# Three raw weight buffers and eight 4 KB tiles, where there were two and ten, in a two-layer hybrid encoder trunk

## The chip, the cores and the metric

The kernel runs on one core of one Trainium2 chip. The metric is the time of one execution in microseconds as the device gives it; the median of three runs is quoted. Of one further execution there is a profile and a trace, and all rows below come from that one. TensorE (PE, with PEld for its weight loads), VectorE (DVE), ScalarE (ACT), GpSimd (POOL) and the DMA queues, nearly all of whose transfers are issued by SyncE (SP), work side by side, and wait for one another by semaphores.

## The reference

Two layers over 256 tokens of width 1024, in float32. Cut to what matters:

```python
def hybrid_layer(h, p_i, ...):
    u = rms_norm(h, g_mix_pre)
    (gq, gk, gv, gg, ra_f, ra_b, aq, ak, av, gate_a, gate_b) = split(u @ w_in)
    o_gla = rms_norm(gla(gq, gk, gv, decay(ra_f)) + gla_backward(gq, gk, gv, decay(ra_b)))
    branch_a = (o_gla * silu(gg)) @ w_o_gla                    # gated linear attention
    branch_b = attention(rope(rms_norm(aq)), rope(rms_norm(ak)), av) @ w_o_attn
    mixed = sigmoid(gate_a) * branch_a + sigmoid(gate_b) * branch_b
    h = h + rms_norm(mixed @ w_out, g_mix_post)
    gate, up = split(rms_norm(h, g_ffn_pre) @ w_ffn_in)        # hidden width 2816
    h = h + rms_norm((silu(gate) * up) @ w_ffn_out, g_ffn_post)
    e = p_i @ w_ple_proj
    return h + rms_norm(sigmoid(h @ w_ple_gate) * e, g_ple_post)
```

Nearly all of the work is in the products with weights, which are read once from memory and used for all 256 tokens.

## The kernel before

**Exactness by three passes.** Each float32 operand of a product is written as a sum of a high part (`wh` for a weight) in the matmul's own float32 format (`fp32r`) and a low part (`wl`), what the rounding left over. A product then is three matmuls: high by high, low by high, high by low (`passes`, line 123, and `mm`, line 107). To make the parts, `split` (line 135) issues two instructions: a copy with rounding on ScalarE (CAST) and a subtraction on VectorE. This holds for weights, and for activations when they have been turned so that the contracted dimension lies on the partitions (`transpose_in`, line 450, by TensorE, or `turn_out` and `take_in`, lines 461 to 474, by a DMA that transposes 16-bit halves, with a copy on ScalarE ahead of it and one behind).

**How weights are streamed.** A weight matrix is cut into units of 128 partitions by 2048 (or 2112) values, 1 MB each. The class `Stream` holds them in a fixed list in the order of use. `Load.start` takes a tile with tag `raw` from the pool `rawp` for a unit, and line 298 issues its DMA on the SP queue. When a unit comes up, `put` takes a `wh` and a `wl` tile from `wp` (four of each), and `fill` issues the casts and subtractions, in two halves of 128 x 1024; then `load` starts the next unit's DMA into a raw buffer. So a raw buffer is filled, cast and subtracted, and a new load into it waits for the subtraction that read it last. `take` gives the next ready pair to the matmuls; `done` gives its place back. At most four units are split and not used up.

Some blocks of weights (the second branch gate, and pairs of FFN blocks) are computed by a scheme of seven products for eight: sums of weight blocks are formed on VectorE (`step`). Their units lie in tiles of the pools `wp` (named `lent`) and `bigp`, not in `rawp`. The change leaves those pools alone.

**Pools.** On chip each partition has room for all pools together: `rawp` (8448 bytes a tile), `wp`, `bigp` (8 KB tiles, nine), `b4p` (4 KB tiles, ten, taken by `mid()`), `smp` (small tiles; four for each tag, where no number is given), and constants. In PSUM `accp` has eight tiles for sums. A tile of `mid()` serves for many things: the norms' scaled rows and squares, the gains that are loaded for them (line 373), the embedding's input `p` (line 1012), the rope table (lines 802 and 803, used by GpSimd in lines 807 to 812), decay weights (`up_weights`, line 828), operands of the linear and the softmax attention, the gated values, and the turned halves of the FFN's hidden activations.

**What sets the order.** The code is written stage by stage: start and rank projections (`0gla`, `0rq`), linear attention (`0gqk`, `0v`, `0gg`), gates and branch projections (`0gate`), merge and output projection (`0merge`, `0wout`), FFN (`0ffnin`, `0ffnout`), embedding (`0ple`), and the same for layer 1. The middle of a tile's name says in which stage it was made, and the first word which kind it is. A list scheduler puts the instructions of each engine and of the SP queue in order: by program order, by priorities (blocks under `high_priority`: the norms, the splits of activations), by its own estimates of when operands and buffers come free, and by explicit `issue_after`. The engines then take their list strictly in order. The number of buffers in a pool therefore changes not only who waits for whom, but also the lists.

**Norms.** `pre_norm` takes a norm ahead of a product: squares and sum (`row_rstd`), the factor 1/rms on GpSimd (lines 534 to 538), the product with the gain (line 542). `post_norm_add` is the norm behind a product: squares (line 522), factor, product with the gain (`vmul`, line 128), and the addition to `h` (line 609). `row_rstd` and `last_norm` each take a small tile `rstd`, of 4 bytes a partition. `outputs`, in the linear attention, takes a small tile `hss`, of 32 bytes. In the last part of an FFN the gated hidden values are made by `vmul` too, into tiles named `t_0ffnin` or `t_1ffnin`, and turned by TensorE or by the transposing DMA.

Of the kernel before, what the change touches and what calls it, by code (L numbers as in the profile page):

```python
# [61 lines left out]
def trunk_kernel(ctx: ExitStack, tc: tile.TileContext, a: dict, out: bass.AP):  # L62
# [8 lines left out]
    PSUM = bass.MemoryType.PSUM  # L71

    cp = ctx.enter_context(tc.tile_pool(name="cp", bufs=1))
    rawp = ctx.enter_context(tc.tile_pool(name="rawp", bufs=2))
    wp = ctx.enter_context(tc.tile_pool(name="wp", bufs=4))
    bigp = ctx.enter_context(tc.tile_pool(name="bigp", bufs=9))
    b4p = ctx.enter_context(tc.tile_pool(name="b4p", bufs=10))
    smp = ctx.enter_context(tc.tile_pool(name="smp", bufs=4))
    accp = ctx.enter_context(tc.tile_pool(name="accp", bufs=8, space=PSUM))

# [423 lines left out]
    def row_rstd(parts, behind=None):  # L504

        ss, r, junk = small(3, "ss"), small(1, "rstd"), mid() if parts[0].shape[-1] > 512 else t512()
        for j, src in enumerate(parts):  # L510
            n = src.shape[-1]
            if j == 2 and behind is not None:
                last_square[0] = nc.vector.scalar_tensor_tensor(
                    out=junk[:, :n], in0=src, scalar=1.0 / 1024.0, in1=src, op0=ALU.mult, op1=ALU.mult,
                    accum_out=ss[:, j : j + 1],
                )
                nc.vector.tensor_scalar(
                    out=r, in0=ss[:, 2:3], scalar1=ss[:, 0:1], scalar2=None, op0=ALU.add
                )
            else:  # L520
                with tc.issue_after(behind.ins) if j and behind is not None else nullcontext():
                    last_square[0] = nc.scalar.activation(
                        junk[:, :n], src, AF.Square, scale=1.0 / 32.0, accum_out=ss[:, j : j + 1]
                    )
            if len(parts) == 3 and j == 1:

                with in_turn():
                    last_pow[0] = nc.gpsimd.tensor_scalar(
                        out=ss[:, 0:1], in0=ss[:, 0:1], scalar1=ss[:, 1:2], scalar2=EPS if behind is not None else 0.0,
                        op0=ALU.add, op1=ALU.add,  # L530
                    )
        with in_turn():
            if behind is None or len(parts) == 2:
                nc.gpsimd.tensor_scalar(
                    out=r, in0=ss[:, 0:1], scalar1=ss[:, len(parts) - 1 : len(parts)], scalar2=EPS,
                    op0=ALU.add, op1=ALU.add,
                )
        last_pow[0] = nc.gpsimd.tensor_tensor(out=r, in0=r, in1=neghalf[:, 0:1], op=ALU.pow)
        return r
# [76 lines left out]
    def last_norm(parts, g, hf):  # L616

        with tc.high_priority(AHEAD):
            yt, junk, ss, r, c = mid(), mid(), small(3, "ss"), small(1, "rstd"), 0
            cuts = []  # L620
            for src in parts:
                cuts.append(slice(c, c + src.shape[-1]))
                c += src.shape[-1]
            nc.scalar.activation(junk[:, cuts[0]], parts[0], AF.Square, scale=1.0 / 32.0, accum_out=ss[:, 0:1])
            nc.vector.scalar_tensor_tensor(
                out=junk[:, cuts[1]], in0=parts[1], scalar=1.0 / 1024.0, in1=parts[1], op0=ALU.mult, op1=ALU.mult,
                accum_out=ss[:, 1:2],
            )
            with in_turn():
                nc.gpsimd.tensor_scalar(  # L630
                    out=ss[:, 2:3], in0=ss[:, 0:1], scalar1=ss[:, 1:2], scalar2=EPS, op0=ALU.add, op1=ALU.add
                )
            total = nc.vector.tensor_tensor_reduce(
                out=junk[:, cuts[2]], in0=parts[2], in1=parts[2], scale=1.0 / 1024.0, scalar=ss[:, 2:3],
                op0=ALU.mult, op1=ALU.add, accum_out=r,
            )
            nc.gpsimd.tensor_tensor(out=r, in0=r, in1=neghalf[:, 0:1], op=ALU.pow)
            yt = [acc(), yt[:, 0:256], acc()[:, 0:256]]
            for j, (src, c) in enumerate(zip(parts, cuts)):
                with tc.issue_after(total.ins) if j else nullcontext():  # L640
                    vmul(yt[j], src, g[:, c])
            for j, c in enumerate(cuts):
                x = h[:, hf, c]
                if j == 1:
                    nc.scalar.activation(yt[j], yt[j], AF.Copy, bias=0.0, scale=r)
                    nc.gpsimd.tensor_tensor(out=x, in0=yt[j], in1=x, op=ALU.add)
                else:
                    nc.vector.scalar_tensor_tensor(out=x, in0=yt[j], scalar=r, in1=x, op0=ALU.mult, op1=ALU.add)
                (nc.scalar if j == 1 else nc.sync).dma_start(out[0, hf * P : (hf + 1) * P, c], x)
# [397 lines left out]
    for l in range(DEPTH):  # L1047
# [332 lines left out]
        def outputs(hf, pr):  # L1380

            o = aux()
            ss = small(8, "hss")
            for i in range(2):
                hd = 2 * pr + i
                c = slice(hd * 256, (hd + 1) * 256)
# [402 lines left out]
```

## Time and profile before

| what | value |
|---|---|
| median of three runs (908.7, 910.29, 912.39) | 910.29 us |
| profiled execution: its time | 908.97 us |
| profiled execution: span, first to last instruction | 907.2 us |
| granted TensorE clock, mean | 0.997 |
| HBM read | 169.50 MB, 190 GB/s over the span |
| layers | layer 1's part is a repetition of layer 0's, less the start |

In the page of the profile a busy time is the time in which an engine worked on an instruction, and "idle before, releaser" tells how long the engine stood ahead of the instructions of a group, and what ended most of it. Rows that begin with two numbers come from a timeline: the first is the start in us from the beginning of the span, the second the time from there to the end of the last of so many instructions in a row (x4), and square brackets hold the wait ahead of them and what ended it. In rows of waits the three numbers are the total in us, the count and the longest. Rows of DMA groups end with the median time from issue to landing. Matmuls are pipelined, so that one can start before the one ahead of it has ended.

### The profile page before, as it was taken

How to read it: one execution, taken by the hardware profiler on the slowest of the kernel's cores; microseconds unless marked ns; L12 is line 12 of the kernel's file. 1: busy time of each engine (PE TensorE's matmuls, PEld its weight loads, DVE VectorE, ACT ScalarE, POOL GpSimd, SP SyncE). 2: the span in 40 equal slices, each digit the busy share in tenths (PEclk: the TensorE clock that was granted, in tenths of full speed). 3: DMA queues.
4: the chain of work that ended last, by engine and by line, in shares of the span. 5: the costliest groups of instructions: out<-in, count | busy, mean ns of one | idle time of the engine just before them, and what ended most of it. 6: DMA issues, size and time to landing. Idle time of an engine off the chain costs nothing.

```text
span 907.2 us, 12121 instructions
## 1 busy us (share of the span) xinstructions
PE 896.5 (99%) x4447; PEld 758.1 (84%) x4447; DVE 791.2 (87%) x1021; ACT 635.3 (70%) x1027; POOL 103.6 (11%) x157
## 2 busy tenths in 40 slices
PE   9999999999999999999999999999999999999997
PEld 8898888878888888877898888888888888888786
DVE  7999989987769989898779899799877799999984
ACT  6688679664569686666676687697645796958563
POOL 3700221300100000000244001110001000000001
PEclk9999999999999999999999999999999999999998
DMA  8654449657497685947575524475574966858461
GB/s 284 219 189 137 140 140 241 212 185 235 139 300 197 211 252 179 285 140 258 183 281 191 182 93 140 139 231 179 193 233 132 312 179 200 249 212 242 144 244 47
DMA packets 116967, 180.25 MB, mean 199 GB/s; under 512 B 30942, under 2 KB 55014, under 8 KB 116396
## 3 DMA queue, kind: packets, MB, share of 16 engines
q1 hardware_dynamic: 116748, 179.35, 61.4%
q8 instruction: 35, 0.57, 0.3%
q14 instruction: 24, 0.20, 0.1%
q10 hardware_dynamic: 160, 0.14, 0.0%
HBM read 169.50 MB, written 3.15 MB: 190 GB/s over the span
## 4 chain that ended last, share of the span: by engine, by line
PE 71%; DVE 14%; DMA 7%; issue 3%; ACT 3%; POOL 0%; POOLq 0%; SPq 0%; ACTq 0%; DVEq 0%
PE acc_1ffnin L123 10%; PE acc_1gate L123 7%; PE acc_0ffnin L123 5%; DVE wl_0ffnin L135 5%; PE acc_1ffnin L107 5%; DVE wl_0gate L135 3%; PE acc_1rq L123 3%; PE acc_0gqk L107 2%; PE acc_1gqk L107 2%; PE acc_1wout L123 2%; PE acc_0ple L123 2%; PE acc_1gg L123 2%; PE acc_1v L123 2%; PE acc_0v L123 2%; PE acc_1merge L123 2%
## 5 line engine op out<-in xcount | busy, mean ns | idle before, releaser
L135 ACT CAST wh_1ffnin<-raw_1ffnin 128x1024 fp32r<-128x1024 f32 x38 | 38.3, 1049 | 21.7 <-DMA raw_1ffnin<-in_w_ffn_out_dram 7.2
L135 DVE TENSOR_TENSOR wl_0ffnin<-raw_0ffnin,wh_0ffnin 128x1024 fp32r<-128x1024 f32 x38 | 44.7, 1221 | 8.5 <-ACT wh_0ffnin L135 8.4
L135 ACT CAST wh_0ffnin<-raw_0ffnin 128x1024 fp32r<-128x1024 f32 x38 | 38.0, 1047 | 19.6 <-DMA raw_0ffnin<-in_w_ffn_out_dram 11.1
L135 DVE TENSOR_TENSOR wl_1ffnin<-raw_1ffnin,wh_1ffnin 128x1024 fp32r<-128x1024 f32 x38 | 44.9, 1220 | 7.6 <-ACT wh_1ffnin L135 7.5
L107 PE MATMUL acc_0ffnin<-wh_0ffnin,big_0ffnin 128*128 128x512 f32 x176 | 45.4, 392 | 0.5 <-DVE big_0ffnin L135 0.5
L107 PE MATMUL acc_1ffnin<-wh_1ffnin,big_1ffnin 128*128 128x512 f32 x176 | 45.2, 390 | 0.0
L123 PE MATMUL acc_1ffnin<-wh_1ffnin,big_1wout 128*128 128x512 f32 x168 | 41.5, 389 | 0.0
L123 PE MATMUL acc_0ffnin<-wh_0ffnin,big_0wout 128*128 128x512 f32 x168 | 41.5, 389 | 0.0
L107 PEld LDWEIGHTS acc_0ffnin<-wh_0ffnin,big_0ffnin 128*128 128x128 f32 x176 | 32.7, 188 | 8.1 <-DVE big_0ffnin L135 0.9
L107 PEld LDWEIGHTS acc_1ffnin<-wh_1ffnin,big_1ffnin 128*128 128x128 f32 x176 | 33.0, 188 | 7.0
L123 PEld LDWEIGHTS acc_1ffnin<-wh_1ffnin,big_1wout 128*128 128x128 f32 x168 | 31.5, 188 | 6.6
L123 PEld LDWEIGHTS acc_0ffnin<-wh_0ffnin,big_0wout 128*128 128x128 f32 x168 | 31.5, 188 | 6.5
L135 DVE TENSOR_TENSOR wl_0ffnin<-lent_0ffnin,wh_0ffnin 128x1024 fp32r<-128x1024 f32 x30 | 35.7, 1220 | 0.6 <-ACT wh_0ffnin L135 0.6
L135 DVE TENSOR_TENSOR wl_1ffnin<-lent_1ffnin,wh_1ffnin 128x1024 fp32r<-128x1024 f32 x30 | 35.6, 1217 | 0.0
L135 ACT CAST wh_1ffnin<-lent_1ffnin 128x1024 fp32r<-128x1024 f32 x30 | 30.3, 1051 | 4.6 <-DVE lent_1ffnin L333 1.5
L135 ACT CAST wh_0ffnin<-lent_0ffnin 128x1024 fp32r<-128x1024 f32 x30 | 30.3, 1050 | 4.4 <-PE acc_0ffnin L123 1.6
L135 DVE TENSOR_TENSOR wl_0gate<-raw_0gate,wh_0gate 128x1024 fp32r<-128x1024 f32 x20 | 24.0, 1246 | 7.9 <-ACT wh_0gate L135 7.9
L135 DVE TENSOR_TENSOR wl_1gate<-raw_1gate,wh_1gate 128x1024 fp32r<-128x1024 f32 x20 | 23.6, 1220 | 7.3 <-ACT wh_1gate L135 7.3
L135 ACT CAST wh_0gate<-raw_0gate 128x1024 fp32r<-128x1024 f32 x20 | 19.8, 1046 | 12.8 <-DMA raw_0gate<-in_w_o_gla_dram 6.7
L135 ACT CAST wh_1gate<-raw_1gate 128x1024 fp32r<-128x1024 f32 x20 | 19.9, 1049 | 11.3 <-DMA raw_1gate<-in_w_o_gla_dram 4.7
L107 PE MATMUL acc_0ffnin<-wl_0ffnin,big_0ffnin 128*128 128x512 f32 x88 | 25.4, 399 | 1.4 <-DVE wl_0ffnin L135 1.4
L107 PE MATMUL acc_1ffnin<-wl_1ffnin,big_1ffnin 128*128 128x512 f32 x88 | 24.5, 395 | 0.6 <-DVE wl_1ffnin L135 0.6
(730 smaller groups left out, 2739.5 us busy)
## 6 DMA issues: line engine op xcount, KB each, us to landing
raw_0ffnin<-in_w_ffn_out_dram SPq DMA_DIRECT2D x11, 1024.0 KB, 6.4
raw_1ffnin<-in_w_ffn_out_dram SPq DMA_DIRECT2D x11, 1024.0 KB, 6.3
lent_0ffnin<-in_w_ffn_in_dram SPq DMA_DIRECT2D x6, 1024.0 KB
lent_1ffnin<-in_w_ffn_in_dram SPq DMA_DIRECT2D x6, 1024.0 KB, 9.0
raw_0v<-in_w_in_dram SPq DMA_DIRECT2D x4, 1024.0 KB, 5.1
raw_0gate<-in_w_o_gla_dram SPq DMA_DIRECT2D x4, 1024.0 KB, 5.9
raw_0gate<-in_w_o_attn_dram SPq DMA_DIRECT2D x4, 1024.0 KB, 5.0
raw_0wout<-in_w_ffn_in_dram SPq DMA_DIRECT2D x8, 512.0 KB, 6.3
```

Of the source, the lines that this page charges most:

```text
L107: return nc.tensor.matmul(o, lhsT, rhs, start=start, stop=stop)
L123: nc.tensor.matmul(o, x, y, start=start and n == 0, stop=stop and n == len(seq) - 1, **kw)
L135: return nc.scalar.copy(hi, src), nc.vector.tensor_tensor(out=lo, in0=src, in1=hi.bitcast(F32), op=ALU.subtract)
```

## The change

The pool of raw weight tiles has three buffers for two, 8448 bytes a partition more; the pool of 4 KB tiles has eight for ten, 8192 bytes less; the two small tags `rstd` and `hss` have two buffers for four. No instruction is added or taken out, and none has other operands than before, but for the buffers in which they lie.

```diff
-    rawp = ctx.enter_context(tc.tile_pool(name="rawp", bufs=2))
+    rawp = ctx.enter_context(tc.tile_pool(name="rawp", bufs=3))
...
-    b4p = ctx.enter_context(tc.tile_pool(name="b4p", bufs=10))
+    b4p = ctx.enter_context(tc.tile_pool(name="b4p", bufs=8))
...
# row_rstd
-        ss, r, junk = small(3, "ss"), small(1, "rstd"), mid() if parts[0].shape[-1] > 512 else t512()
+        ss, r, junk = small(3, "ss"), small(1, "rstd", 2), mid() if parts[0].shape[-1] > 512 else t512()
...
# last_norm
-            yt, junk, ss, r, c = mid(), mid(), small(3, "ss"), small(1, "rstd"), 0
+            yt, junk, ss, r, c = mid(), mid(), small(3, "ss"), small(1, "rstd", 2), 0
...
# outputs
-            ss = small(8, "hss")
+            ss = small(8, "hss", 2)
```

The order on the engines changes in many places. Three of them follow: rows with a minus stand there before, rows with a plus now, rows with neither in both.

The first is the SP queue in the gate stage of layer 0. `raw_0gate_...` are weight units (the number tells tiles apart), `mid_0gg_...` are transposed activations, `ggla` is a gain, and the rows L802 and L803 load the rope table; loads of gains and of `p` (L373, L1012) follow some rows further on, ahead of where raw_0gate_1890 stood.

```order
 L467 DMA_TRANSPOSE mid_0gg_1646<-big_0gg_1276 128x8x128 x2
-L298 DMA raw_0gate_1686<-in_w_o_gla_dram 128x4x512
+L298 DMA raw_0gate_1731<-in_w_o_gla_dram 128x4x512
 L373 DMA ggla_1gla_4912<-in_g_gla_out_dram 128x256
-L298 DMA raw_0gate_1731<-in_w_o_gla_dram 128x4x512
 L298 DMA raw_0gate_1803<-in_w_in_dram 128x4x512
+L298 DMA raw_0gate_1890<-in_w_o_gla_dram 128x4x512
 L802 DMA mid_0merge_2268<-in_rope_cos_dram 128x2x128
 L803 DMA mid_0merge_2268<-in_rope_sin_dram 128x2x128
```

Each weight unit stands one place earlier in the sequence of units: raw_0gate_1890 now comes before the rope table, where it came behind it and the loads that follow.

The second is the SP queue in the FFN of layer 0, at the last blocks of hidden values. `raw_` and `lent_` are weight units, and the transpositions turn the gated values for the output product.

```order
 L298 DMA raw_0ffnin_3376<-in_w_ffn_out_dram 128x2x1024
+L298 DMA raw_0ffnin_3396<-in_w_ffn_out_dram 128x2x1024
 L298 DMA lent_0ffnin_3390<-in_w_ffn_in_dram 128x4x512
 L298 DMA lent_0ffnin_3394<-in_w_ffn_in_dram 128x4x512
-L298 DMA raw_0ffnin_3396<-in_w_ffn_out_dram 128x2x1024
+L298 DMA raw_0ffnin_3445<-in_w_ffn_in_dram 128x4x512
 L467 DMA_TRANSPOSE t_0ffnin_3434<-mid_0ffnin_3155 128x8x128
-L298 DMA raw_0ffnin_3445<-in_w_ffn_in_dram 128x4x512
 L467 DMA_TRANSPOSE t_0ffnin_3460<-mid_0ffnin_3463 128x8x128
```

raw_0ffnin_3445 stood between the two transpositions and now stands ahead of both.

The third is VectorE at the end of the FFN of layer 1. `wl_` are subtractions for weight units, `t_1ffnin_...` are gated values that TensorE turns next, and `big_1ffnin_7700` are their low parts behind the turn.

```order
 L135 TENSOR_TENSOR wl_1ffnin_7601<-raw_1ffnin_7554,wh_1ffnin_7600 128x1024 x2
+L135 TENSOR_TENSOR wl_1ffnin_7633<-raw_1ffnin_7592,wh_1ffnin_7632 128x1024 x2
 L128 TENSOR_TENSOR t_1ffnin_7652<-mid_1ffnin_7458,t_1ffnin_7652 128x512
-L135 TENSOR_TENSOR wl_1ffnin_7633<-raw_1ffnin_7592,wh_1ffnin_7632 128x1024 x2
+L135 TENSOR_TENSOR wl_1ffnin_7656<-raw_1ffnin_7606,wh_1ffnin_7655 128x1024 x2
+L135 TENSOR_TENSOR big_1ffnin_7700<-aux_1ffnin_7695,big_1ffnin_7700 128x4x128
 L131 TENSOR_TENSOR mid_1ffnin_7457<-acc_1ffnin_7460,mid_1ffnin_7458 128x512
-L135 TENSOR_TENSOR big_1ffnin_7700<-aux_1ffnin_7695,big_1ffnin_7700 128x4x128
+L135 TENSOR_TENSOR wl_1ffnin_7680<-raw_1ffnin_7638,wh_1ffnin_7679 128x1024
 L128 TENSOR_TENSOR t_1ffnin_7676<-mid_1ffnin_7458,t_1ffnin_7676 128x512
-L135 TENSOR_TENSOR wl_1ffnin_7656<-raw_1ffnin_7606,wh_1ffnin_7655 128x1024 x2
```

The subtractions of one more weight unit now stand ahead of each of the two products t_1ffnin_7652 and t_1ffnin_7676.

## The prediction

> **What bounds the kernel now.** I read the page's busy line first, then the waits of TensorE, ScalarE and the SP queue, and last the timelines of the few places where TensorE really stands.
>
> ```profile
> PE 896.5 (99%) x4447; PEld 758.1 (84%) x4447; DVE 791.2 (87%) x1021; ACT 635.3 (70%) x1027; POOL 103.6 (11%) x157
> L107 PE MATMUL acc_0ffnin<-wl_0ffnin,big_0ffnin 128*128 128x512 f32 x88 | 25.4, 399 | 1.4 <-DVE wl_0ffnin L135 1.4
> PE acc_1ffnin L107 <- DVE wl_1ffnin L135: 0.6, 2, 0.4
> PE acc_0gate L123 <- ACT wh_0gate L135: 0.3, 1, 0.3
> ```
>
> TensorE is busy for 896.5 of the span's 907.2 us. No change to buffers takes a matmul out, so what can be won is only the time in which TensorE stands, and the rows show that to be small: 1.4 us of waits for `wl` in the FFN of layer 0, 0.6 us in layer 1, 0.3 us in the gate. But the end of a matmul is modelled here, with 0.399 us for one that can be followed much sooner, so idle time behind a matmul is understated. I count starts instead. Below, a block of five runs for 1.32 us; less the modelled 0.39 of the last, four steps of **0.23 us** are left, and what lies between two starts beyond 0.23 us per matmul is standing.
>
> ```profile
> SPq L298 <- DVE wl_0ffnin L135: 77.3, 19, 9.2
> ACT wh_0ffnin L135 <- DMA raw_0ffnin<-in_w_ffn_out_dram: 11.1, 3, 5.7
> ACT mid_0ffnin L474 <- DMA t_0ffnin<-mid_0ffnin: 6.2, 5, 2.7
> raw_0ffnin<-in_w_ffn_out_dram SPq DMA_DIRECT2D x11, 1024.0 KB, 6.4
> ```
>
> Two raw buffers do hold the loads back: in the FFN of layer 0 the SP queue waits 77.3 us, 19 times, for the subtraction that frees a buffer. Yet of that only 11.1 us reach ScalarE, as three waits for a landed unit, and 1.4 us reach TensorE. Cast and subtraction run ahead of the matmuls, and this lead swallows most late loads. So the question is local: where has the lead been used up?
>
> ```profile
> 182.75 0.61 PE L123 MATMUL acc_0gate<-wl_0gate,mid_0gate 128*128 128x512 f32 x2
> 183.62 1.68 PE L123 MATMUL acc_0gate<-wh_0gate,big_0gg 128*128 128x512 f32 x6 [0.25 <-ACT wh_0gate L135]
> ...
> 386.16 0.63 PE L107 MATMUL acc_0ffnin<-wl_0ffnin,big_0ffnin 128*128 128x512 f32 x2
> 387.04 0.74 PE L107 MATMUL acc_0ffnin<-wl_0ffnin,big_0ffnin 128*128 128x512 f32 x2 [0.25 <-DVE wl_0ffnin L135]
> 387.61 0.63 PE L107 MATMUL acc_0ffnin<-wh_0ffnin,big_0ffnin 128*128 128x512 f32 x2
> ...
> 399.64 0.84 PE L107 MATMUL acc_0ffnin<-wh_0ffnin,big_0ffnin 128*128 128x512 f32 x3
> 400.74 0.73 PE L107 MATMUL acc_0ffnin<-wl_0ffnin,big_0ffnin 128*128 128x512 f32 x2 [0.26 <-DVE wl_0ffnin L135]
> 401.87 0.73 PE L107 MATMUL acc_0ffnin<-wl_0ffnin,big_0ffnin 128*128 128x512 f32 x2 [0.40 <-DVE wl_0ffnin L135]
> 402.44 0.85 PE L107 MATMUL acc_0ffnin<-wh_0ffnin,big_0ffnin 128*128 128x512 f32 x3
> ...
> 415.64 1.16 PE L107 MATMUL acc_0ffnin<-wl_0ffnin,big_0ffnin 128*128 128x512 f32 x4
> 417.26 1.20 PE L107 MATMUL acc_0ffnin<-wh_0ffnin,big_0ffnin 128*128 128x512 f32 x4 [0.47 <-DVE big_0ffnin L135]
> ...
> 419.78 0.63 PE L107 MATMUL acc_0ffnin<-wl_0ffnin,big_0ffnin 128*128 128x512 f32 x2
> 420.67 0.73 PE L107 MATMUL acc_0ffnin<-wl_0ffnin,big_0ffnin 128*128 128x512 f32 x2 [0.26 <-DVE wl_0ffnin L135]
> ...
> 847.49 0.61 PE L107 MATMUL acc_1ffnin<-wh_1ffnin,big_1ffnin 128*128 128x512 f32 x2
> 848.26 0.73 PE L107 MATMUL acc_1ffnin<-wl_1ffnin,big_1ffnin 128*128 128x512 f32 x2 [0.16 <-DVE wl_1ffnin L135]
> 849.39 0.73 PE L107 MATMUL acc_1ffnin<-wl_1ffnin,big_1ffnin 128*128 128x512 f32 x2 [0.40 <-DVE wl_1ffnin L135]
> 849.96 1.32 PE L107 MATMUL acc_1ffnin<-wh_1ffnin,big_1ffnin 128*128 128x512 f32 x5
> ```
>
> Beyond 0.23 us a matmul, TensorE stands here for: gate 0.87 - 0.46 = 0.41; 386 to 387.6, four matmuls, 1.45 - 0.92 = 0.53; 399.6 to 402.4, seven, 2.80 - 1.61 = 1.19; 415.6, four, 1.62 - 0.92 = 0.70; 419.8, two, 0.89 - 0.46 = 0.43; layer 1, six, 2.47 - 1.38 = 1.09. Together **4.35 us**, 0.5% of the time: all that the larger waits on weights cost.
>
> The Trainium skill (Perfetto Trace Analysis, section Identifying Performance Opportunities) says that the same gap repeating on the engine that should be saturated can mean too little SBUF for the next tile. The trace agrees only for the SP queue, with its 19 waits; the gaps of TensorE do not repeat.
>
> **The change part by part.** *The third buffer* moves each load one unit earlier; the work is the same, and the gain is what the places above give up.
>
> ```profile
> 382.47 1.17 ACT L474 COPY mid_0ffnin<-t_0ffnin 128x1024 uint16<-128x1024 uint16 x1 [2.67 <-DMA t_0ffnin<-mid_0ffnin]
> ...
> 384.62 2.36 DVE L135 TENSOR_TENSOR wl_0ffnin<-raw_0ffnin,wh_0ffnin 128x1024 fp32r<-128x1024 f32 x2 [2.23 <-ACT wh_0ffnin L135]
> ```
>
> At 386 the root is not the weight unit itself. ScalarE waits 2.67 us for a turned tile whose transposition was issued behind a 1 MB load (raw_0ffnin_3445 between t_0ffnin_3434 and t_0ffnin_3460 in the order), VectorE therefore stands 2.23 us, and from there to 402 it has no time to catch up. In the changed order that load stands ahead of both transpositions and may start when the subtraction two units back is done, some 4 us sooner; the second transposition then no longer queues behind it. The casts and subtractions behind 382.47 come about 2 us sooner, more than the longest single hold-up of 0.6 us at 401.3, so 0.53 + 1.19 go. With the same lead the two units after 402 land before they are cast, and 0.70 + 0.43 go. In layer 1 the same pair of transpositions stands before 848: 1.09 goes. In the gate raw_0gate_1890 is issued at 176.0, after a run of small loads, and moves ahead of them: 0.41 goes. I take the whole **-4.35**.
>
> The Trainium skill (DMA: Bandwidth & Descriptors, section Queues, rings and completion order) says that each DMA engine takes the descriptors of a ring in order. By that rule the load now ahead of t_0ffnin_3434 could hold up that first transposition as it held up the second; the wait of 2.67 us agrees with the rule, and the second rival below is what it would give.
>
> *What is late next.* A cast and a subtraction that are ready sooner are also put ahead of other work.
>
> ```profile
> L135 ACT CAST wh_0ffnin<-raw_0ffnin 128x1024 fp32r<-128x1024 f32 x38 | 38.0, 1047 | 19.6 <-DMA raw_0ffnin<-in_w_ffn_out_dram 11.1
> L135 DVE TENSOR_TENSOR wl_0ffnin<-raw_0ffnin,wh_0ffnin 128x1024 fp32r<-128x1024 f32 x38 | 44.7, 1221 | 8.5 <-ACT wh_0ffnin L135 8.4
> ...
> 855.72 2.36 DVE L135 TENSOR_TENSOR wl_1ffnin<-raw_1ffnin,wh_1ffnin 128x1024 fp32r<-128x1024 f32 x2
> 858.00 0.68 DVE L128 TENSOR_TENSOR t_1ffnin<-mid_1ffnin,t_1ffnin 128x512 f32<-128x512 f32 x1
> ...
> 860.43 0.60 PE L450 MATMUL aux_1ffnin<-ident,t_1ffnin 128*128 128x128 f32 x4
> ```
>
> At the end of the FFN of layer 1 two more subtractions (wl_1ffnin_7633) now come before the product t_1ffnin_7652, which TensorE turns at 860.43. The subtraction row at 855.72 comes 0.9 us sooner with the rest, but the product then starts after 2 x 2.36 us of subtractions instead of one: 854.8 + 4.7 = 859.5, its end 860.2, against 860.43 - 1.09 = 859.3 at which TensorE now wants it: **+0.9**, and about +0.2 at the second turned half, which three more places of subtraction precede. In layer 0 the whole chain is 2.2 us sooner at this point, so the same two subtractions cost only about **+0.3**.
>
> *Eight 4 KB tiles for ten.* No row of before shows a wait for a 4 KB tile. In the changed program I find three new ones of any length.
>
> ```profile
> 147.48 1.89 DVE L135 TENSOR_TENSOR mid_0gate<-mid_0gate,mid_0gate 128x512 fp32r<-128x512 f32 x3
> ...
> 169.24 0.43 SPq L373 DMA_DIRECT2D mid_0wout<-in_g_ffn_pre_dram  x1
> 176.00 10.36 SPq L298 DMA_DIRECT2D raw_0gate<-in_w_o_gla_dram  x2
> 179.62 3.21 POOL L812 TENSOR_TENSOR rope_0merge<-mid_0merge 128x64 f32<-128x64 f32 x4
> ```
>
> The cast of mid_0gate_1701 must wait for the subtractions at 147.48 and is put six places later on ScalarE, into a stretch without idle time: 0.65 us of work there, of which I charge **+0.2** in each layer (nothing if the lead holds, 0.65 if none). The gain load mid_0wout_2287, at 169.24, must wait for GpSimd's last product, at 182.8, and stops the SP queue for 13.6 us. Behind it stand the load of `p` and the second raw_0gate, which before was issued at about 186 (176.00 + 10.36) anyway; raw_0gate_1890 stands ahead: 0. The zero fill for the next layer's decay weights comes 13.6 us later on GpSimd, and these are used more than 10 us after that: 0. Casts moved ahead of the attention's exponentials at 50 to 70 us find ScalarE idle, waiting for loads, but make two subtractions precede the scores' operands: I charge **+0.25** per layer (0 to 1.2, one subtraction).
>
> *The two-buffer small tiles* (`rstd`, `hss`) hold 4 bytes and 32 bytes a partition and are read within one norm; their previous user is over ten us back: 0, and one GpSimd instruction of some 0.6 us if not.
>
> **Sum:** -4.35 + 0.9 + 0.2 + 0.3 + 0.4 + 0.5 = **-2.05 us**, on the profiled execution 908.97 - 2.05 = 906.9 (span 907.2, with 1.8 us around it). The median of the runs, 910.29, lies 1.3 us above that execution and inside their spread of 908.7 to 912.39, so against the median I say **908.2**.
>
> **Rivals.** *The gain comes whole and more.* If the new costs vanish in other idle time, -4.35 is left, and with waits of the same kind under 0.2 us at other places (the 0.5 us for `big_0ffnin` is counted, the rest of the 907.2 - 896.5 is not) up to 6: about 905.2. For it: ScalarE stands 30% of the time. Against: VectorE, at 87%, is the one that releases TensorE in five of the six places. It is what the skill's rule on repeating gaps would give.
>
> *The wait only moves.* If the load that now leads holds up the first transposition as it did the second, the chain from 382 to 402, and its like in layer 1, start no sooner: 0.53, 1.19 and 1.09 stay, -1.54 + 2.3 = +0.8, 911.1. The same comes if the third buffer is filled no sooner because the SP queue itself is stopped. For it: the queue takes all in order, and a load takes 6.4 us to land. Against: the transposition is issued about 3 us after the load's new place.
>
> *Slower: weight work ahead of the norms.*
>
> ```profile
> 709.14 1.41 DVE L542 SCALAR_TENSOR_TENSOR mid_1wout<-h,rstd_1wout,mid_1wout 128x512 f32<-128x512 f32 x2 [0.85 <-POOL rstd_1wout L538]
> ...
> 709.94 0.66 PE L450 MATMUL aux_1wout<-ident,mid_1wout 128*128 128x128 f32 x4
> ```
>
> The first half of this norm ends at 709.14 + 0.75 and TensorE turns it at 709.94: nothing to spare. There are twelve such norms (after the output projection, the FFN and the embedding, two token halves, two layers). Each cast and subtraction that slips ahead of one costs 1.05 + 1.22 = 2.27 us less the chain's slack, and it decides from the point where that slack is under 2.27. With four norms hit it is +9.1 - 2.05, 917.3. Against: at 709 the casts that move ahead come out of ScalarE's way later (they ran before the squares already), so this one I find no later. For: the scheduler's order is set without these measured times.
>
> **How the numbers follow.** My forecast has a chance of 0.42, with a range of its own of 906 to 910.5; whole gain 0.18; moved wait 0.18; slower 0.22. A measurement of this kernel tells 0.5% from no change, 4.6 us here: faster is under 905.7, slower over 914.8. Most of the first rival and an edge of the forecast is faster: 0.19. Most of the slower rival is over 914.8: 0.2. The rest, 0.61, is within. The range of 8 in 10 must reach into both outer cases, and takes in the two bounds of the 0.65 and 1.2 us terms: 904.8 to 916.5.
>
> **What would show it.** Right: no idle time at 386 to 402 and 848, ScalarE's wait at L474 under 1 us, raw_0gate_1890 landed before 180; a new wait of TensorE for `t_1ffnin` at its turn near 860; the SP queue's waits for subtractions far under 77 us while TensorE's busy time stays. Wrong: TensorE waiting at L450 for a norm (slower), or ScalarE waiting at L474 for the first transposition (moved). The forecast fails if the chain of VectorE from 384 to 402 is as full as before and starts no sooner.

## The result, and the profile after

The changed kernel takes **906.3 us** (median of 13 runs, 904.55 to 907.59) against 910.29 us (median of 13 runs, 906.48 to 912.39): a ratio of 0.9965, with a 95% interval of 0.9951 to 0.9978 (the two medians alone give 0.9956, which lies inside it). That is 2 to 4.5 us less, a gain that is real and smaller than the 4.6 us that the prediction called its border. The forecast was 908.2: the direction and the range held, and the measured median lies 1.9 us under it.

The profiled execution took 906.67 us, its span is 904.9 us. The page and the groups by line answer the first rows that the prediction showed.

```profile
PE 895.2 (99%) x4447; PEld 760.0 (84%) x4447; DVE 789.9 (87%) x1021; ACT 634.9 (70%) x1027; POOL 105.0 (12%) x157
L107 PE MATMUL acc_0ffnin<-wl_0ffnin,big_0ffnin 128*128 128x512 f32 x88 | 24.1, 391 | 0.0
```

The same matmuls on `wl` that waited 1.4 us in all now wait for nothing. In the timeline of TensorE, the place from 399 to 402 runs without a break: the block of eight takes 1.98 us, and 1.98 less the last one's 0.39 is seven steps of 0.227.

```profile
400.68 1.07 PE L107 MATMUL acc_0ffnin<-wl_0ffnin,big_0ffnin 128*128 128x512 f32 x4
401.58 1.98 PE L107 MATMUL acc_0ffnin<-wh_0ffnin,big_0ffnin 128*128 128x512 f32 x8
```

What TensorE still waits for is in the table of its waits, and in this execution it is other things than weights. The second column is what it waited for, then the total in us, the count, the longest.

```profile
PE aux_1wout L450 <- DVE mid_1wout L542: 0.5, 1, 0.5
PE aux_1emb L1020 <- DMA mid_0ffnout<-in_p_dram: 0.4, 1, 0.4
PE acc_0rq L107 <- ACT wh_start L144: 0.4, 1, 0.4
PE acc_0gqk L107 <- DVE mid_0at L135: 0.2, 1, 0.2
```

The waits of the SP queue hold two surprises. Its waits for the subtractions of the FFNs are hardly shorter in layer 0 (77.3 us before) and longer in layer 1 (73.1 us before), and there is a new stop for GpSimd.

```profile
SPq L298 <- DVE wl_1ffnin L135: 83.0, 17, 14.5
SPq L298 <- DVE wl_0ffnin L135: 76.1, 20, 9.4
SPq L373 <- POOL rope_0merge L812: 11.5, 1, 11.5
```

To compare whole executions I take, for each of the 4447 matmuls and transpositions, the time from the start of the one ahead of it, and subtract the step that the same shape takes in a closed run (0.226 us for 512 columns, and in the same way for others). What is left, summed by stage, is the standing of TensorE. A step taken 0.001 us longer would make each total some 3.6 us smaller, so only the differences between columns count. Since one execution is little, each kernel has two: the runs `again` and `after_again` below are the same two kernels once more.

| standing, us | before | again | changed | after_again |
|---|---|---|---|---|
| start (0rq) | 0.93 | 1.62 | 2.00 | 1.57 |
| attention and decay operands, layer 0 (0gqk, 0at) | 0.57 | 0.57 | 1.51 | 1.53 |
| gates, layer 0 | 0.64 | 0.55 | 0.45 | 1.30 |
| merge, layer 0 | 0.59 | 0.76 | 0.23 | 0.18 |
| FFN, layer 0, and its end (0ffnin, 0ffnout) | 4.66 | 3.17 | 0.60 | 0.61 |
| embedding of layer 1 | 0.00 | 0.13 | 0.63 | 0.00 |
| output projection, layer 1 | 0.40 | 0.81 | 0.93 | 0.90 |
| FFN, layer 1 | 1.63 | 3.28 | 0.67 | 0.44 |
| all stages | 13.73 | 15.27 | 11.29 | 10.93 |

The two FFNs give 5.0 us (before against changed) and 5.4 us (again against after_again), all stages together 2.4 and 4.3 us. So 2.6 and 1.1 us are given back. The attention of layer 0 takes 0.95 us of that in both pairs. The rest lies in rows that differ by up to 0.85 us between two executions of the same kernel (the start, the gates, the embedding, the output projection), so two executions do not tell how much of it is the change's.

### The profile page after: what moved, and what is told of

Its sections match the earlier page's. It is cut to its first block, busy times and chain, and to the rows that moved or that the text cites. A ratio compares the mean times of both kernels' runs of the same rounds, so it can differ in the third digit from the quotient of the medians.

```text
span 904.9 us, 12163 instructions
## 1 busy us (share of the span) xinstructions
PE 895.2 (99%) x4447; PEld 760.0 (84%) x4447; DVE 789.9 (87%) x1021; ACT 634.9 (70%) x1027; POOL 105.0 (12%) x157
## 4 chain that ended last, share of the span: by engine, by line
PE 85%; DVE 6%; ACT 3%; DMA 3%; issue 2%; POOL 1%; SPq 0%; POOLq 0%; ACTq 0%; DVEq 0%
PE acc_0ffnin L123 12%; PE acc_1ffnin L123 11%; PE acc_1gate L123 7%; PE acc_1ffnin L107 7%; PE acc_0ffnin L107 6%; PE acc_1rq L123 3%; PE acc_1gqk L107 2%; PE acc_0wout L123 2%; PE acc_0v L123 2%; PE acc_1gg L123 2%; PE acc_1v L123 2%; PE acc_0merge L123 2%; PE acc_1merge L123 2%; PE acc_1ple L123 2%; PE acc_0gg L123 2%
## 5 line engine op out<-in xcount | busy, mean ns | idle before, releaser
L135 ACT CAST wh_1ffnin<-raw_1ffnin 128x1024 fp32r<-128x1024 f32 x38 | 38.6, 1049 | 17.4 <-PE acc_1ffnin L107 9.0
L135 ACT CAST wh_0ffnin<-raw_0ffnin 128x1024 fp32r<-128x1024 f32 x38 | 38.6, 1049 | 16.6 <-PE acc_0ffnin L107 7.6
L135 DVE TENSOR_TENSOR wl_0ffnin<-raw_0ffnin,wh_0ffnin 128x1024 fp32r<-128x1024 f32 x38 | 44.8, 1220 | 3.8 <-ACT wh_0ffnin L135 3.8
L135 DVE TENSOR_TENSOR wl_1ffnin<-raw_1ffnin,wh_1ffnin 128x1024 fp32r<-128x1024 f32 x38 | 44.8, 1220 | 2.4 <-ACT wh_1ffnin L135 2.4
L135 DVE TENSOR_TENSOR wl_1ffnin<-lent_1ffnin,wh_1ffnin 128x1024 fp32r<-128x1024 f32 x30 | 35.8, 1220 | 2.2 <-ACT wh_1ffnin L135 2.2
L135 DVE TENSOR_TENSOR wl_0ffnin<-lent_0ffnin,wh_0ffnin 128x1024 fp32r<-128x1024 f32 x30 | 35.7, 1219 | 1.6 <-ACT wh_0ffnin L135 1.6
L135 ACT CAST wh_1ffnin<-lent_1ffnin 128x1024 fp32r<-128x1024 f32 x30 | 30.6, 1049 | 8.5 <-PE acc_1ffnin L107 3.9
L135 ACT CAST wh_0ffnin<-lent_0ffnin 128x1024 fp32r<-128x1024 f32 x30 | 30.6, 1052 | 6.1 <-PE acc_0ffnin L107 3.9
L135 DVE TENSOR_TENSOR wl_0gate<-raw_0gate,wh_0gate 128x1024 fp32r<-128x1024 f32 x20 | 24.6, 1265 | 4.0 <-ACT wh_0gate L135 3.9
L135 ACT CAST wh_0gate<-raw_0gate 128x1024 fp32r<-128x1024 f32 x20 | 20.2, 1053 | 8.1 <-DMA raw_0gate<-in_w_o_attn_dram 3.5
L135 DVE TENSOR_TENSOR wl_1gate<-raw_1gate,wh_1gate 128x1024 fp32r<-128x1024 f32 x20 | 23.6, 1221 | 1.5 <-ACT wh_1gate L135 1.4
L135 ACT CAST wh_1gate<-raw_1gate 128x1024 fp32r<-128x1024 f32 x20 | 20.1, 1048 | 6.4 <-PE acc_1gate L123 3.5
```

The source lines that it names most:

```text
L135: return nc.scalar.copy(hi, src), nc.vector.tensor_tensor(out=lo, in0=src, in1=hi.bitcast(F32), op=ALU.subtract)
```

## The experiments

The theory was that in the FFNs a weight load stood between two transpositions in the SP queue and made the second late, and that the third buffer moves this load ahead. The rivals were: the third buffer's lead swallows late transpositions wherever the load stands; and the fewer 4 KB tiles do something of their own, for good or ill.

**again** is the kernel before, once more.

> The kernel before, unchanged, for a second profile of it: how far the places and lengths of TensorE's standing repeat from execution to execution. If the places are set by the order, the same six places show, each within 0.3 us of the first profile, and the span lies within 2 us of 907.2. If they come from the spread of the loads' landing times, other places show.

It took 910.58 us, span 908.5. The waits of TensorE on weights repeat in kind, not in place:

```profile
PE acc_1ffnin L107 <- DVE wl_1ffnin L135: 1.7, 3, 0.9
PE acc_0ffnin L107 <- DVE wl_0ffnin L135: 0.7, 2, 0.4
PE acc_0ffnin L107 <- DVE big_0ffnin L135: 0.5, 1, 0.5
```

The standing at 386 is not there, and there is one of 1.6 us at 789 in layer 1. Those at 184, 401, 416, 420 and 850 are. The norm at 709, which I had taken as free of waits, stands 0.5 us. The order of the instructions is the same in both, so it sets where TensorE can stand; where it does stand I put down to the spread of landing times (the load ahead of the second transposition landed at 381.43 in before and at 380.87 in again), which no run isolates. **after_again** says the same of the changed kernel:

> The changed kernel, unchanged, for a second profile. Standing that the change sets shows again at the same place: 56 (0.5 us), 196 (0.3 us), 438 (0.6 us), 863 (0.2 us), and none in the FFN from 386 to 421 and at 848. What the spread of landing times sets, at the start (5.5) and at the norm of layer 1 (708), may be longer or shorter by up to 1 us.

It took 906.23 us, span 904.5: 56 and 196 again, nothing in the FFN from 386 to 417 nor at 848, but not 438 nor 863, and 1.1 us at 197 where 0.3 had been.

**two_raw** takes the third buffer back and leaves the rest of the change:

```diff
-    rawp = ctx.enter_context(tc.tile_pool(name="rawp", bufs=3))
+    rawp = ctx.enter_context(tc.tile_pool(name="rawp", bufs=2))
```

> The changed kernel with two raw buffers in place of three, so that only the eight 4 KB tiles and the small tiles are left of the change. Theory A, the gain is the third buffer's alone and the fewer tiles cost next to nothing: within 0.6 us of before (ratio 0.9995 to 1.0007), TensorE stands at 386 to 402 and at 848 as before, and the SP queue's wait for the subtractions of layer 0's FFN stays near 77 us. Theory B, fewer 4 KB tiles bring part of the gain by another order: below before by 1 us or more (ratio under 0.999). Theory C, the eight tiles have a hidden cost that the third buffer covers: over before by 1 us or more.

It took **920.63 us**, ratio to before 1.0136 (1.0123 to 1.0149): theory C, by a size that I had not on my list. The loss is one place. In the FFNs nothing is gained: the SP queue waits 77.2 us for the subtractions of layer 0's, and TensorE waits 0.6 us for `wl` in layer 0 and 1.2 us in layer 1, so the fewer tiles alone do not remove those waits. The place is in the gate of layer 0. These are the SP queue, GpSimd, ScalarE and TensorE there, in the timeline of two_raw, and then three windows with the busy times of PE, PEld, DVE, ACT and POOL, the granted clock, and the share and GB/s of the DMA engines:

```profile
168.94 0.43 SPq L373 DMA_DIRECT2D mid_0wout<-in_g_mix_post_dram  x1
179.07 4.19 POOL L812 TENSOR_TENSOR rope_0merge<-mid_0merge 128x64 f32<-128x64 f32 x4
183.29 0.33 SPq L373 DMA_DIRECT2D mid_0wout<-in_g_ffn_pre_dram  x1
184.19 0.42 SPq L298 DMA_DIRECT2D raw_0gate<-in_w_o_gla_dram  x1
191.27 2.94 ACT L135 CAST wh_0gate<-raw_0gate 128x1024 fp32r<-128x1024 f32 x3 [15.39 <-DMA raw_0gate<-in_w_o_gla_dram]
192.36 2.08 PE L123 MATMUL acc_0gate<-wh_0gate,big_0gg 128*128 128x512 f32 x4 [8.96 <-ACT wh_0gate L135]
```

```profile
170.00:183.00 13.00, 13.00 (x59) 10.76 (x58) 12.97 (x10) 4.46 (x6) 9.67 (x10) 1.00 0.25 88
183.00:192.30 9.30, 0.41 (x2) 0.00 (x0) 0.12 (x1) 1.03 (x2) 0.26 (x1) 0.64 0.57 197
192.30:196.00 3.70, 3.64 (x9) 2.87 (x10) 3.66 (x4) 3.70 (x5) 0.00 (x0) 0.51 0.03 9
```

With eight tiles, the load of the FFN's pre-norm gain gets the tile of the rope table, and must wait until GpSimd has used it, at 183.3. The SP queue takes its list in order, so the weight load behind it, raw_0gate_1890, goes out at 184.19 and not at 176.00 as before; it lands at 191.2 (182.4 before), and TensorE stands 9 us. Behind that the clock is at 0.51 for 3.7 us, so that nearly half of it is lost as well, another 1.8 us (3.7 x 0.49). This is the stop that the prediction saw at 169.24 and priced at nothing, because raw_0gate_1890 stands ahead of it in the changed kernel.

**mid9** asks whether this needs any other order: it is the kernel before with nine tiles, and on every engine its list is that of before, row for row.

```diff
-    b4p = ctx.enter_context(tc.tile_pool(name="b4p", bufs=10))
+    b4p = ctx.enter_context(tc.tile_pool(name="b4p", bufs=9))
```

> The kernel before with nine 4 KB tiles in place of ten, nothing else; every engine has the same instructions in the same order as before, and the only difference is which earlier user a tile waits for. Theory A, one tile less is enough for the stop: the load of p (L1012) now waits for GpSimd's last rope product, and raw_0gate_1890 stands right behind it, so TensorE stands 8 to 10 us at about 192 and runs at half speed for 3 to 4 us behind it: 918 to 921, ratio 1.010 to 1.014. Theory B, the loss of two_raw came from its other order of casts and subtractions in the gate: no difference from before, ratio 0.999 to 1.001.

It took 917.99 us, ratio 1.0097 (1.0077 to 1.0117), just under the lower edge of what theory A had set, and far from theory B; TensorE stands 6.5 us where theory A had 8 to 10. Here it is the load of `p` that waits for GpSimd:

```profile
180.35 3.21 POOL L812 TENSOR_TENSOR rope_0merge<-mid_0merge 128x64 f32<-128x64 f32 x4
183.59 0.38 SPq L1012 DMA_DIRECT2D mid_0wout<-in_p_dram  x1
184.06 9.31 SPq L298 DMA_DIRECT2D raw_0gate<-in_w_o_gla_dram  x2
190.64 2.93 PE L123 MATMUL acc_0gate<-wh_0gate,big_0gg 128*128 128x512 f32 x6 [6.52 <-ACT wh_0gate L135]
```

One tile of 4 KB less, no instruction moved, 8.7 us lost. **unblock** then takes two_raw and puts only that gain load behind the weight load:

```diff
-        gpre = gain(a["g_ffn_pre"][l], mid(), D)
+        with tc.issue_after(sent[123].ins) if l == 0 else nullcontext(): gpre = gain(a["g_ffn_pre"][l], mid(), D)
```

(`sent[123]` is the DMA of raw_0gate_1890.)

> Two raw buffers, eight 4 KB tiles and the small tiles of the change, as in two_raw, but the load of the FFN's pre-norm gain of layer 0 is put behind the weight load raw_0gate_1890 in the SP queue, by an order constraint alone. Theory A, the loss of two_raw is one place: that gain load waits for GpSimd's rope products and stops the queue with the weight load behind it. Then the standing of 9.1 us at 192 in the gate goes, and with it the half-speed matmuls behind it (1.6 us): 920.6 - 10.7 = 909.9, ratio to before 0.9995 to 1.002. Theory B, eight tiles are short in many places: under half of the loss goes, the ratio stays over 1.006.

It took 910.91 us, ratio 1.0006 (0.999 to 1.0022): theory A, 1 us over what it had set. In this kernel's table TensorE's wait at the place is 0.7 us:

```profile
PE acc_0gate L123 <- ACT wh_0gate L135: 0.7, 1, 0.7
```

So the fewer tiles cost 10 to 12 us (by the medians and by the ratios) through one wait in one queue, and nothing that can be told elsewhere.

**between** keeps all of the change, but puts the one load of each FFN back between the two transpositions:

```diff
-                        nc.sync.dma_start(dst, src)
+                        with tc.issue_after(turns[-1].ins) if len(self.loads) in (84, 8) else nullcontext(): nc.sync.dma_start(dst, src)
```

(84 and 8 units are left when these two loads are issued; `turns[-1]` is the first transposition.)

> The changed kernel, three raw buffers, with one load a layer (raw_0ffnin_3445, raw_1ffnin_7360) put back between the two transpositions in the SP queue, by an order constraint alone. Theory A, the root in the FFN is a transposition that queues behind a 1 MB load: the second transposition lands 2 us or more later than in the changed kernel, ScalarE waits over 1.5 us for it at L474, and 1.5 to 2.8 us of the gain is lost (ratio to before 0.9985 to 0.9996). Theory B, the lead that the third buffer gives to all units swallows that wait: ScalarE waits at L474, but TensorE does not stand, and the time stays within 0.6 us of the changed kernel (ratio to before near 0.9965).

It took 906.33 us, ratio 0.9975 (0.996 to 0.9989): not to be told from the changed kernel, though the interval also reaches into theory A's range. The profile decides. The second transposition lands at 380.5 (378.3 in the changed kernel), and ScalarE waits 1.20 us for it at L474, less than the 1.5 us that theory A had set; the first row, 2.18 us, is a wait for the first transposition, whose copy now stands earlier in ScalarE's list. The timeline of between:

```profile
375.60 1.17 ACT L474 COPY mid_0ffnin<-t_0ffnin 128x1024 uint16<-128x1024 uint16 x1 [2.18 <-DMA t_0ffnin<-mid_0ffnin]
380.52 1.18 ACT L474 COPY mid_0ffnin<-t_0ffnin 128x1024 uint16<-128x1024 uint16 x1 [1.20 <-DMA t_0ffnin<-mid_0ffnin]
383.49 2.35 DVE L135 TENSOR_TENSOR wl_0ffnin<-raw_0ffnin,wh_0ffnin 128x1024 fp32r<-128x1024 f32 x2
```

In the changed kernel both copies run without a wait:

```profile
377.48 2.26 ACT L474 COPY mid_0ffnin<-t_0ffnin 128x1024 uint16<-128x1024 uint16 x2
```

But the subtraction behind them in between, at 383.49, has no wait ahead of it (2.23 us in the profile of before), and TensorE stands nowhere from 386 to 402. It does stand some 0.6 us more than in the changed kernel a little later, at 411.6 and 417.1, where it turns the gated values:

```profile
PE aux_0ffnin L450 <- DVE t_0ffnin L128: 0.3, 1, 0.3
```

My theory A falls here: of its 1.5 to 2.8 us at most 0.6 is there, so with three buffers the place of that load does not decide. Whether those 0.6 us come from the late transposition or from the spread is open.

**hold** is the other half: the kernel before, two buffers, ten tiles, and the load held back until the second transposition is issued.

```diff
-            while self.loads and (self.lend or
+            while self.loads and len(turns) >= held.get(len(self.loads), 0) and (self.lend or
...
-        nc.sync.dma_start_transpose(out=words.rearrange("p (x t) -> p x t", t=P), in_=planes)
+        turns.append(nc.sync.dma_start_transpose(out=words.rearrange("p (x t) -> p x t", t=P), in_=planes)); ws.start() if len(turns) in (13, 26) else None
```

(`held` is {85: 13, 9: 26}; the line with `issue_after` of between is in this kernel too.)

> The kernel before, two raw buffers and ten tiles, with the same one load a layer held back until the second transposition is issued. Theory A, the queue position of that load is the root: the wait of 2.67 us at L474 goes, the standing at 386 to 402 and at 848 goes with it (-1.7 and -1.1 us), 2 to 2.8 us under before (ratio 0.9969 to 0.998), with no third buffer. Theory B, the third buffer is needed because later loads are late too: the standing only moves to the next late unit (402 to 421 in layer 0), and under 1 us is won (ratio over 0.999).

It took 905.83 us, ratio 0.9975 (0.9961 to 0.9989): theory A. SP queue, ScalarE and the load, in the timeline of hold; the second transposition lands at 377.7 where it had been 382.4:

```profile
371.15 4.69 SPq L467 DMA_TRANSPOSE t_0ffnin<-mid_0ffnin  x2
375.88 0.58 SPq L298 DMA_DIRECT2D raw_0ffnin<-in_w_ffn_in_dram  x1
376.57 2.38 ACT L474 COPY mid_0ffnin<-t_0ffnin 128x1024 uint16<-128x1024 uint16 x2
```

By the rows of the table, the standing of the two FFNs falls to 0.66 and 0.58 us, with two buffers. The edit reaches beyond the SP queue: the scheduler also put the second copy (L474) right behind the first on ScalarE, with the split behind it, and moved a low part on VectorE. What hold shows is the new place together with this, not the place alone. One new wait takes 1.7 us of the gain in the profiled execution:

```profile
PE aux_1emb L1020 <- DMA mid_0ffnout<-in_p_dram: 1.7, 1, 1.7
```

**hold_late** turns `p` two ticks later for that (`embed(l + 1, 5)` for `embed(l + 1, 3)`).

> The kernel hold, two raw buffers and ten tiles with one load a layer behind the second transposition, and the turn of p for layer 1's embedding two ticks later. Theory A, the 1.8 us at 438 in hold are a wait for the load of p alone, and go: 1 to 1.8 us under hold, ratio to before 0.9955 to 0.9975. Theory B, the wait moves to the next turn: no difference from hold.

It took 906.55 us, ratio 0.9979 (0.9963 to 0.9994). The wait is gone from the profile, but the time is not to be told from hold's; in its profiled execution the start alone stands 1.2 us more than in hold's (2.80 and 1.64 us). The price of that wait stays open.

**big8** has the third buffer with all ten 4 KB tiles, and pays with one of the 8 KB tiles:

```diff
-    bigp = ctx.enter_context(tc.tile_pool(name="bigp", bufs=9))
-    b4p = ctx.enter_context(tc.tile_pool(name="b4p", bufs=8))
+    bigp = ctx.enter_context(tc.tile_pool(name="bigp", bufs=8))
+    b4p = ctx.enter_context(tc.tile_pool(name="b4p", bufs=10))
```

> Three raw buffers with all ten 4 KB tiles; the space comes from the pool of 8 KB tiles, which has eight in place of nine. Theory A, the third buffer makes the whole gain and the fewer 4 KB tiles only cost: no stop of the SP queue for GpSimd in the gate of layer 0, TensorE stands at none of the FFN places, time 905 to 906.5 (ratio to before 0.9945 to 0.9975). Theory B, a pool of 8 KB tiles that is one short costs in its place: new waits for big tiles, ratio over 0.999.

It took 905.79 us, ratio 0.9965 (0.9951 to 0.9978): theory A. The queue has no stop for GpSimd, the standing of the gate is 0.00 and that of the FFNs 0.58 and 0.66 us. The attention of layer 0 still stands 1.33 us, and in two_raw, with eight tiles and two buffers, it stands no longer than in before, so that price comes with the third buffer and not with the fewer 4 KB tiles.

**combined** and **keys_first** try to better the changed kernel by order alone: combined puts the gain load of the FFN's norm behind two weight loads and the turn of `p` three ticks later, keys_first also gives the splits of queries and keys a priority.

```diff
-        gpre = gain(a["g_ffn_pre"][l], mid(), D)
+        with tc.issue_after(sent[121].ins) if l == 0 else nullcontext(): gpre = gain(a["g_ffn_pre"][l], mid(), D)
...
-            embedding = embed(l + 1, 3)
+            embedding = embed(l + 1, 6)
```

The second part is in keys_first alone, and stands there for the keys in the same way:

```diff
-                split(qh, ql, ps)
+                with tc.high_priority(100): split(qh, ql, ps)
```

> The changed kernel with two of its new waits taken out by order alone: the load of the FFN's pre-norm gain of layer 0 goes behind two weight loads, so that its wait for GpSimd stops no weights, and the turn of p for layer 1's embedding is put three ticks later. Theory A, these waits are on TensorE's path: the standing at 196 (0.4 us) and at 438 (0.2 to 0.6 us) goes, 0.6 to 1.0 us under the changed kernel, ratio to before 0.9945 to 0.997. Theory B, they are covered elsewhere or come back at the next place: no difference from the changed kernel that can be told.

> The kernel combined, and the splits of the attention's queries and keys under a priority, so that their low parts come ahead of weight subtractions on VectorE. Theory A, the standing of 0.5 to 0.8 us at 55 to 60 is the price of weight subtractions put ahead of the scores' operands, and goes: 0.6 us under combined, ratio to before 0.994 to 0.9965. Theory B, the subtractions that are put back are late in their turn, and TensorE waits for wl in the projections at 50 to 70: no gain or a loss.

combined took 904.87 us, ratio 0.9957 (0.9943 to 0.9972), the lowest median of all. Its profile has neither wait (standing 0.00 in the gate and at the embedding, 9.32 in all), but its interval overlaps that of the changed kernel, so the gain is seen in the profile and not in the times. keys_first took 905.01 us, ratio 0.9954 (0.9939 to 0.9969): no gain over combined. The wait at 56 is gone, and this is what came for it:

```profile
PE acc_0v L123 <- DVE mid_0at L135: 1.2, 1, 1.2
```

It is again a low part of the attention, one stage on (theory B had expected a weight's).

## Why the prediction was right, and where it was not

**The bound** was right: no matmul went, and all that moved is the standing of TensorE.

**The -4.35 for the third buffer.** In the FFNs I had 2.85 us in layer 0 and 1.09 in layer 1, from the larger waits of one execution. By the sums of the table the two executions of before stand 4.66 and 3.17 us there in layer 0, and 1.63 and 3.28 in layer 1; after the change 0.6 and 0.4 to 0.7 are left. So the term of the FFNs is -5.0 to -5.4, not -3.94: I had counted one execution, and only its larger breaks. The 0.41 of the gate did not go. raw_0gate_1890 landed at 173.4 (I had said before 180), but the next unit, the second raw_0gate of the prediction's row at 176.00, then stands behind the stop for GpSimd and lands at 195.2, and TensorE stands 0.3 us at 196 for it, and 1.1 us in after_again.

**Its mechanism in the FFN** was half right. The load now stands ahead of both transpositions, the second lands at 378.3 and not at 382.4, and ScalarE's wait of 2.67 us is gone. By the Trainium skill (DMA: Bandwidth & Descriptors, section Queues, rings and completion order) that load could have held up the first transposition. The trace agrees that it lands behind the load, at 377.4 after 376.6; but in the kernel before it had a load ahead of it as well and landed at 377.9, so nobody waited longer, and this rival did not come here. A long wait for a transposition is there at the first one of each FFN, where it costs nothing. ScalarE's waits in the changed kernel:

```profile
ACT mid_0ffnin L474 <- DMA t_0ffnin<-mid_0ffnin: 4.6, 3, 3.7
ACT mid_1ffnin L474 <- DMA t_1ffnin<-mid_1ffnin: 3.5, 3, 2.8
```

The longest of layer 0 ends at 318.70 (the same copy waited 0.37 us before), that of layer 1 at 763.48. TensorE stands for neither: a wait longer than the 2.67 us of 382 has no price there. But `between` shows that three buffers don't need the new place, and `hold` that the new place, with the order that the scheduler made for it, doesn't need three buffers. Either of the two frees VectorE's chain at 384.

**The +0.9, +0.2 and +0.3 at the ends of the FFNs** were too much: 0 at the first turn of layer 1, at most 0.2 at the second, and none at the first turn of layer 0. The step that failed is "the subtraction row at 855.72 comes 0.9 us sooner with the rest". VectorE and TensorE in the changed kernel:

```profile
852.27 4.63 DVE L135 TENSOR_TENSOR wl_1ffnin<-raw_1ffnin,wh_1ffnin 128x1024 fp32r<-128x1024 f32 x4
856.82 0.69 DVE L128 TENSOR_TENSOR t_1ffnin<-mid_1ffnin,t_1ffnin 128x512 f32<-128x512 f32 x1
857.66 0.60 PE L450 MATMUL aux_1ffnin<-ident,t_1ffnin 128*128 128x128 f32 x4
```

The four subtractions do stand ahead of the product, but they begin 3.45 us sooner, and the product ends at 857.5, just in time. I had let VectorE gain only as much as TensorE, though its own wait for the late cast (1.17 us at 832.14 before) was gone as well.

**The +0.4 for casts in the gates** was 0: the gate of layer 1 stands 0.00 us.

**The +0.5 for the attention** had the right mechanism and the wrong shape: 0.95 us more in layer 0, nothing in layer 1. VectorE has four subtractions in a row there, and the low parts of the queries come behind them. The first two rows are from before, where one subtraction precedes the first low part, the other three from the changed kernel:

```profile
48.74 1.22 DVE L135 TENSOR_TENSOR wl_0kv<-raw_0rq,wh_0kv 128x1024 fp32r<-128x1024 f32 x1
49.88 0.68 DVE L135 TENSOR_TENSOR mid_0at<-aux_0at,mid_0at 128x512 fp32r<-128x512 f32 x1
49.80 4.62 DVE L135 TENSOR_TENSOR wl_0kv<-raw_0rq,wh_0kv 128x1024 fp32r<-128x1024 f32 x4
54.34 0.69 DVE L135 TENSOR_TENSOR mid_0at<-aux_0at,mid_0at 128x512 fp32r<-128x512 f32 x1
56.00 0.73 PE L107 MATMUL acc_0gqk<-big_start,wh_0kv 128*128 128x512 f32 x2 [0.21 <-DVE mid_0at L135]
```

**The sum.** By the means of the table the change is worth -3.4 us: -5.2 in the FFNs, +0.95 in the attention, and some +0.9 in rows that vary from execution to execution, such as the embedding (0.63 us in one execution, 0.00 in the other), for which the prediction had no term. Its gain of 4.35 was too small. Its costs of 2.3 are near the 1.8 or so that came back, but half of that came at places that it had not named, and the ends of the FFNs, with 1.4 of the 2.3, cost next to nothing; that the costs agree in total is luck.

**The stop of the SP queue, priced at 0,** was nearly right for the changed kernel, where it costs the 0.3 to 1.1 us at 196, and hid its largest number. Without the third buffer it costs 10 to 12 us; the third buffer pays for it by having one more unit on its way. By the ratios (1.0136 and 0.9965) the change is a loss of 12 us and a gain of 15 to 16, most of which meet in one place, and "0" was the difference of the two. The prediction named the wait, what was queued behind it, and why it did not count, and should have priced it with that cover gone.

**The rivals.** The whole gain and more, 4.35 to 6 us, had the size of what the FFNs give (5.0 to 5.4), but the costs did not vanish. Weight work ahead of the norms (slower) was not to be excluded by my argument: at 708 TensorE stands 0.6 us in both executions of the changed kernel. In before it is 0 in the first execution and 0.5 us in the second, so at most a part of it is the change's.

**What would show it.** The sign that failed is "the SP queue's waits for subtractions far under 77 us". They are 76.1, and in layer 1 they grew from 73.1 to 83.0. My reading, which no run isolates, is that a queue that loads ahead as far as buffers allow ends in a wait for a buffer however many there are, and that one more buffer only moves each wait one unit earlier. What went is ScalarE's wait for landed units at L135, 11.1 us before. In the changed kernel the same group waits most for TensorE to give back a split tile:

```profile
L135 ACT CAST wh_0ffnin<-raw_0ffnin 128x1024 fp32r<-128x1024 f32 x38 | 38.6, 1049 | 16.6 <-PE acc_0ffnin L107 7.6
```

The other sign, a wait at L474 under 1 us, held at 382 and not at 318.7.

## What to carry to other kernels

The number of buffers in a pool also decides which earlier user each tile waits for: before taking a tile from a pool, list the loads that then wait for a slow engine and see what stands behind them in the same DMA queue (`mid9` lost 8.7 us by one such wait, with no instruction moved). Price every wait that is "covered" with its cover gone as well, because a net 0 can be a loss and a gain of over 10 us each. Before paying for a buffer, see whether the order of a few transfers gives the same: here moving one load a layer came to 0.9975, and the third buffer to 0.9965, which cannot be told apart. And judge a prefetch buffer by the consumers' waits, never by the queue's own, and by more than one execution where single waits are half a microsecond.

## What the runs showed of the hardware

After 9 us of standing in two_raw the granted clock was 0.51 for 3.7 us; in mid9, after 6.5 us, matmuls of 512 columns stepped at 0.43 us instead of 0.23 until 196.3, 5.6 us long (granted clock 0.51 from 190.6 to 196.3). By the sums of standing, the slow matmuls add 1.8 us to 9.1 in two_raw and 2.7 to 6.7 in mid9. The Trainium skill (TensorE: Matmul & The Clock Gate, Part 1: The HAM clock gate (the "warmup" mystery)) has the half clock after at least one idle window of about 3.4 us and full speed after at least one busy window of the same length, and it calls the window free-running. Both kernels agree with "at least": 3.7 and 5.6 us are each more than one window and less than two.

A transposition that is issued behind a 1 MB load landed 0.8 to 1.1 us after that load in four cases (382.44 after 381.43 in before, 381.72 after 380.87 in again, 380.50 after 379.45 in between, 377.40 after 376.56 in the changed kernel), whether it had been issued 2 or 4 us behind it. It is not always so short: the first of the pair in again landed at 378.14, 2.4 us after the load ahead of it (375.71). With no load on its way, one took 3.1 us from issue to landing (292.27 to 295.37 in before).

GpSimd's last four rope products took 3.21 us in mid9 and before, 4.19 in two_raw and 6.16 in the changed kernel, where VectorE's subtractions and an addition of two weight blocks ran beside them all the time; what sets this was not tried.
